# A scaled residual: the first norm's root goes into the merged tiles and x ahead of the output projection

## The chip, the cores and the metric

The kernel runs on one core of a Trainium2 chip. The metric is the device time of one execution in microseconds (us); below 1 us durations are also given in nanoseconds (ns). The kernel before takes 1426.54 us, the median of three runs (1425.07, 1426.54, 1426.93). One execution was recorded by the hardware profiler; it took 1428.4 us, and its span, from the first recorded instruction to the last, is 1426.7 us.

Five engines work side by side, each through its own instructions in order: PE (matrix products), DVE and ACT (element by element), POOL and SP (here they mostly issue DMA transfers: POOL the stores, SP the loads). PEld is PE's loading of the stationary operand.

## The reference, cut to what matters

One decoder layer over x of 1024 tokens by 1024 channels, in float32:

```
u = rms_norm(x, norm1_g)
z_pool, z_lru, z_gelu, z_gate = split(u @ w_in)
y_pool = causal_multiscale_pool(z_pool) @ pool_proj
y_lru  = rglru_branch(z_lru, z_gelu) @ lru_proj
gates  = sigmoid(z_gate + b_gate)                       # two gates per channel
merged = gates[0] * y_pool + gates[1] * y_lru
h = x + merged @ w_out
v = rms_norm(h, norm2_g)
g_ff, u_ff = split(v @ w_ffn_in)
h = h + (silu(g_ff) * u_ff) @ w_ffn_out
h = h + sigmoid(rms_norm(h, ple_norm_g) @ w_ple_gate) * (p @ w_ple_proj)
return rms_norm(h, final_g)

rms_norm(x, g) = x * rsqrt(mean(x * x, over channels) + 1e-6) * g
```

## The kernel before, in words

**Layout.** Activations lie transposed: a tile has 128 channels on the partitions and the 1024 tokens beside one another, in float32; LOW and HIGH are its halves of 512 tokens. A row vector over the tokens, such as a norm's root, is spread to all partitions by PE (`spread`, L367: 16 small matmuls) and copied by ACT (L371) into a tile of the tag `rstd`; `rep1` is that of the first norm, `rep2` that of the second. `norm1.r` and `n2.r` are small columns with the roots themselves.

**Products in two parts.** Every operand of PE is kept as a hi part, which ACT makes by a cast (`hi`, L115), and a lo part, the rest, which DVE makes by a subtraction behind that cast (`lo`, L119). A product takes three matmuls: L219, L220 and L221 (L227 in plain projections). L220 needs the activation's lo part, L221 the weight's. A Strassen scheme with seven products runs over pairs of tiles; a unit is 12 matmuls (k = 0 to 3, three each) over the four operands of one kind: B11, T1, T2, B21, T3, B22, T4 in that order. The operands of T1, T2, T4 and the weight sums come from DVE first (L194 for weights, L400 to L406 for activations). Products that make up one output go to ACT (copies `z`, L497 to L509) and DVE (adds L499 to L507).

**Stages.** Input projection; pooling and LRU branches; the LRU's projection (L227, eight tiles, `done_lru(m)` behind each: two multiplications L933 of the gate with the PE bank, an add L934: merged tile m); the output projection (two groups of two pairs of tiles, 14 units each, 561 to 657 us), the input projection of the channel mixer (`w_fin`), its output projection (`w_fout`, three chunks), and the end with the embedding gate and the last norm.

**The residual.** When an output tile m of the output projection is finished, `residual(m)` adds it to x, loaded by SP into a tile `xr` (L970, DVE), stores the sum, makes `v` from it, the sum times `norm2_g` and `rep1` (L974, DVE), puts the making of `v`'s operands into the background, and adds the square (L327, ACT) to `ss` (L328, DVE; the first tile's square is written to `ss` itself, L324). The second norm's root is taken from `ss` at the sixth product of the next stage; `ratio` (L1001, L1002) divides the first norm's root out again, which is in `v` already.

**What sets the order.** The program is written out when it is built, and each engine keeps that order. `drive` goes through the units: for each it first issues the loads of later weights on SP, then the lo part (`second`) and the hi part (`first`) of weights up to three units ahead, then some steps of the background, then the unit's matmuls, and at the next unit what follows on them (`post`: copies, adds, residuals). The background is a queue of small generators of which the first two are stepped in turn, by a credit of 0.5 us per us of PE work; `some_operands(acts, k, names)` is one, and makes the operands named for one k as soon as its tiles are there. What is not made so early is made by `prepare`, one kind ahead of its use. `force(key)` steps the background until something has been issued.

**The last projection.** In chunk 1 of `w_fout` the class `Residual` loads the stored sums into `hr` and adds them (L1082) when the seventh product of a tile is in. The bank additions are L1079.

Of the kernel before, what the change touches and what calls it, by code (L numbers as in the profile page):

```python
# [64 lines left out]
def hybrid_block(ctx: ExitStack, tc: tile.TileContext, xT, pT, vec, w_in, w_rgig, w_pool,  # L65
# [264 lines left out]
    class Rstd:  # L330
# [8 lines left out]
        def sums(self, last=None):  # L339

            n = self.n
            m = ps()
            for i in range(n):
                t = self.t0 + i * P
                pe.matmul(m[:, i:i + 1], self.ss[:, t:t + P], mean, start=True, stop=last is None)
                if last is not None:
                    pe.matmul(m[:, i:i + 1], last[:, i * P:(i + 1) * P], mean, start=False, stop=True)
            sm = cp.tile([P, 3, 8], F32, name="sm", tag="sm", bufs=3)
            v, r, t = (sm[:, i, :n] for i in range(3))
            dve.tensor_scalar(v, m[:, :n], EPS, None, ALU.add)  # L350
            act.activation(t, v, AF.Sqrt)
            dve.reciprocal(r, t)
            dve.tensor_mul(t, r, r)
            dve.tensor_mul(t, t, v)
            dve.tensor_scalar(t, t, -0.5, 1.5, ALU.mult, ALU.add)
            dve.tensor_mul(r, r, t)
            self.v, self.r = v, r
# [562 lines left out]

    def pre_lru(m, a):
        if m == 0 and a == 0:
            force(*[("y", "op", c) for c in range(4)])
            load_gate(8)
# [5 lines left out]
    def done_lru(m, banks):  # L930
# [3 lines left out]
        dve.tensor_add(g, g, t0.pop(m))  # L934
        if m % 2 == 0:
            ma.a[m // 2] = g
            background.append(some_operands(ma, m // 2, ("B11", "T1")))
        else:
            ma.b[m // 2] = g
            background.append(some_operands(ma, m // 2, ("T2", "B21")))  # L940
# [8 lines left out]
    def load_xr(m):  # L949
        xr[m] = at("xr")  # L950
        nc.sync.dma_start(xr[m], xT[m])
# [3 lines left out]
    def loads_of_group(m0):  # L955
        def pre(q, j, size):
            i = QS.index(q)
            if m0 == 0:
                if i == 0 and j == 0:
                    state["ss2"] = at("ss")  # L960
                    state["rep1"] = norm1.spread()
# [5 lines left out]
    def residual(m):  # L967
        def then(z):
# [3 lines left out]

            v = at("v")
            dve.scalar_tensor_tensor(v, h, col(C_G2, m), state["rep1"], ALU.mult, ALU.mult)  # L974
# [20 lines left out]
    def pre_fin(q, j, size):  # L995
        prepare_v(q, j, size)
        if q == 5 and j == 0:
            state["norm2"].sums()
            n2 = state["norm2"]
            ratio = cp.tile([P, 8], F32, name="ratio")  # L1000
            dve.reciprocal(ratio, norm1.r)  # L1001
            dve.tensor_mul(ratio, ratio, n2.r)  # L1002
            state["ratio"] = ratio
        if q == 7 and j == 0:
            state["rep2"] = state["norm2"].spread(state["ratio"])
# [53 lines left out]
    class Residual:  # L1059
# [12 lines left out]
        def __call__(self, q, bank):  # L1072
            h = hs[2 * self.i], hs[2 * self.i + 1]
            for t, s in {1: ((0, LOW),), 2: ((0, LOW),), 6: ((0, HIGH),), 3: ((0, HIGH),),
# [6 lines left out]
                if not self.left[t] and self.c == 1:  # L1081
                    dve.tensor_add(h[t], h[t], self.h[t])  # L1082
# [39 lines left out]
    for c, (k0, k1) in enumerate(CHUNKS):  # L1122
        def pre_fout(q, j, size, c=c):
            chunks[c].load_some()

# [160 lines left out]
```

## Time and profile before

| | |
|---|---|
| median of three runs | 1426.54 us |
| profiled execution, its span | 1428.4 us, 1426.7 us |
| PE busy | 1363.4 us, 96% |
| DVE busy | 1074.8 us, 75% |
| ACT busy | 697.7 us, 49% |
| output projection, 561 to 700 us | PE 119.14 us busy, mean clock 0.94 |
| DMA moved | 220.56 MB |

How to read it: busy times are sums over instructions, and PE's are modelled at their ends, so a busy PE need not be at its peak. The clock is what was granted of 2.4 GHz, as a share; 0.50 is 1.2 GHz. In a timeline a row has its start, its duration, the engine and line, the operation with out<-in, the shape, a count if several rows are joined, and in brackets how long the engine was idle before it and what ended that. Starts of neighbours on one engine lie closer together than their durations say, since they overlap a little.

### The profile page before, as it was taken

What the parts mean: (1) busy time and instruction counts of PE and PEld (TensorE: products, weight loads), DVE (VectorE), ACT (ScalarE), POOL (GpSimd) and SP (SyncE); (2) the same over time, 40 slices, a digit from 0 to 9 for tenths busy, and PEclk for the clock granted to TensorE, in tenths of its full rate; (3) what the DMA queues carried; (4) which work ended last, traced back from release to release, by engine and by line L of the source; (5) the groups of instructions that cost most, each with busy time, mean ns of one, the idle gap of its engine ahead of it and who ended that gap; (6) DMA issues with size and microseconds to landing.
All of it is one profiled execution on the core that took longest, in us unless ns stands there. A gap on an engine that the chain in (4) does not pass through costs nothing.

```text
span 1426.7 us, 16476 instructions
## 1 busy us (share of the span) xinstructions
PE 1363.4 (96%) x5958; PEld 1117.1 (78%) x5958; DVE 1074.8 (75%) x1583; ACT 697.7 (49%) x1114; POOL 86.5 (6%) x194
## 2 busy tenths in 40 slices
PE   6999999999999999977999999999999999999986
PEld 4787888888788888756788888888888877887865
DVE  5977788888775556778798888888787856768566
ACT  6558665877866122443554444444444521226331
POOL 0003010010000000000001000111110100000000
PEclk7999999999999999989999999999999999999997
DMA  7122143333559221332024444444567798813103
GB/s 311 74 78 97 58 153 110 122 124 109 193 197 364 89 89 38 110 138 98 16 89 148 148 162 148 162 163 163 192 233 268 277 419 303 343 66 126 62 28 118
DMA packets 64738, 220.56 MB, mean 155 GB/s; under 512 B 7312, under 2 KB 9872, under 8 KB 64656
## 3 DMA queue, kind: packets, MB, share of 16 engines
q1 hardware_dynamic: 45936, 151.80, 30.0%
q0 software_dynamic: 18576, 67.64, 11.7%
q8 instruction: 47, 0.77, 0.2%
q14 instruction: 35, 0.29, 0.1%
q10 hardware_dynamic: 144, 0.06, 0.0%
HBM read 147.65 MB, written 71.83 MB: 154 GB/s over the span
## 4 chain that ended last, share of the span: by engine, by line
PE 78%; DVE 11%; ACT 5%; issue 3%; DMA 2%; POOL 1%; DVEq 0%; SPq 0%; ACTq 0%; POOLq 0%
PE ps L221 22%; PE ps L220 22%; PE ps L219 22%; PE ps L227 11%; DVE w L119 2%; DVE ss L328 1%; DVE v L974 1%; DMA wr<-w_fout 1%; DVE xr L970 1%; DMA lT<-fT 1%; DVE wr L194 1%; PE ps L367 1%; DVE xB L119 1%; ACT w L115 1%; DVE xT L119 1%
## 5 line engine op out<-in xcount | busy, mean ns | idle before, releaser
L115 ACT CAST w<-wr 128x512 fp32r<-128x512 f32 (+2 forms) x384 | 227.1, 609 | 362.6 <-DVE wr L194 252.2
L119 DVE TENSOR_TENSOR w<-wr,w 128x512 fp32r<-128x512 f32 (+2 forms) x384 | 256.5, 672 | 52.6 <-ACT w L115 51.9
L221 PE MATMUL ps<-xT,w 128*128 128x512 f32 x704 | 276.3, 392 | 9.9 <-DVE w L119 9.9
L220 PE MATMUL ps<-xT,w 128*128 128x512 f32 x704 | 275.9, 392 | 3.4 <-DVE xT L119 3.4
L219 PE MATMUL ps<-xT,w 128*128 128x512 f32 x704 | 276.0, 392 | 0.1
L220 PE MATMUL ps<-xB,w 128*128 128x512 f32 x528 | 207.6, 393 | 9.3 <-DVE xB L119 9.1
L219 PE MATMUL ps<-xB,w 128*128 128x512 f32 x528 | 206.7, 392 | 2.1 <-ACT xB L115 1.2
L221 PE MATMUL ps<-xB,w 128*128 128x512 f32 x528 | 206.9, 392 | 0.0
L221 PEld LDWEIGHTS ps<-xT,w 128*128 128x128 f32 x704 | 133.1, 189 | 40.3 <-DVE w L119 12.7
L220 PEld LDWEIGHTS ps<-xT,w 128*128 128x128 f32 x704 | 133.1, 189 | 32.5 <-DVE xT L119 5.0
L219 PEld LDWEIGHTS ps<-xT,w 128*128 128x128 f32 x704 | 133.1, 189 | 28.4 <-ACT w L115 0.7
L220 PEld LDWEIGHTS ps<-xB,w 128*128 128x128 f32 x528 | 99.8, 189 | 32.2 <-DVE xB L119 11.8
L219 PEld LDWEIGHTS ps<-xB,w 128*128 128x128 f32 x528 | 99.8, 189 | 23.8 <-ACT xB L115 1.6
L221 PEld LDWEIGHTS ps<-xB,w 128*128 128x128 f32 x528 | 100.0, 189 | 21.1 <-DVE w L119 0.6
L227 PE MATMUL ps<-y,w 128*128 128x512 f32 x384 | 87.2, 389 | 0.0
L227 PEld LDWEIGHTS ps<-y,w 128*128 128x128 f32 x384 | 72.1, 188 | 15.0
L1079 DVE TENSOR_TENSOR h<-h,ps 128x512 f32<-128x512 f32 x68 | 46.5, 684 | 42.6 <-PE ps L221 42.4
L194 DVE TENSOR_TENSOR wr<-wr 128x512 f32<-128x512 f32 (+1 forms) x112 | 76.0, 679 | 3.1 <-DMA wr<-w_fout 1.1
L219 PE MATMUL ps<-lT,w 128*128 128x512 f32 x176 | 68.9, 392 | 3.4 <-DMA lT<-fT 2.6
L221 PE MATMUL ps<-lT,w 128*128 128x512 f32 x176 | 68.7, 390 | 0.0
L220 PE MATMUL ps<-lT,w 128*128 128x512 f32 x176 | 68.5, 389 | 0.0
L115 ACT CAST w<-s 128x512 fp32r<-128x512 f32 (+1 forms) x56 | 34.3, 613 | 57.3 <-DVE s L194 57.3
(218 smaller groups left out, 2145.0 us busy)
## 6 DMA issues: line engine op xcount, KB each, us to landing
wr<-w_fin SPq DMA_DIRECT2D x44, 512.0 KB, 5.7
fT<-xT POOLq DMA_DIRECT2D x44, 512.0 KB, 5.2
lT<-fT SPq DMA_DIRECT2D x44, 512.0 KB, 8.7
wr<-w_in SPq DMA_DIRECT2D x36, 512.0 KB, 4.1
fB<-xB POOLq DMA_DIRECT2D x33, 512.0 KB, 5.7
lB<-fB SPq DMA_DIRECT2D x33, 512.0 KB, 7.7
g<-z POOLq DMA_DIRECT2D x16, 512.0 KB, 2.9
g<-g SPq DMA_DIRECT2D x16, 512.0 KB, 6.4
```

Of the source, the lines that this page charges most:

```text
L115: act.copy(op[:, :x.shape[1]], x)
L119: dve.tensor_tensor(op[:, H:H + n], x, op[:, :n].bitcast(F32), ALU.subtract)
L194: f(self.place(out), self.place(a), self.place(b))
L219: pe.matmul(bank, a, xop[:, :H], start=first, stop=False, skip_group_check=more)
L220: pe.matmul(bank, a, xop[:, H:], start=False, stop=False, skip_group_check=more)
L221: pe.matmul(bank, b, xop[:, :H], start=False, stop=last, skip_group_check=more)
L227: pe.matmul(bank, w, xop[:, s], start=f, stop=e)
L328: dve.tensor_add(ss, ss, sq)
L367: pe.matmul(bank[:, i * P:(i + 1) * P], r[:, b + i:b + i + 1].broadcast_to([P, P]), ident, start=True, stop=True)
L970: dve.tensor_add(h, h, z)
L974: dve.scalar_tensor_tensor(v, h, col(C_G2, m), state["rep1"], ALU.mult, ALU.mult)
L1079: dve.tensor_add(h[t][:, s], h[t][:, s], bank)
```

## The change

The root of the first norm is multiplied into the merged tiles (`done_lru`, new L959) and into x (`scaled_x`, new L932) ahead of the output projection. x is scaled tile by tile in the background, each tile loaded once more, multiplied and stored to DRAM (`xs`), from where the residual loads it. The residual's sum is thus scaled, its square goes into the second norm, with the epsilon scaled by the root's square (`eps1`), `ratio` is not needed any more, and `v` is the sum times `norm2_g` alone, made by ACT (new L1002). In chunk 1 of the last projection the stored sum is multiplied by the inverse root (`inv1`, new L1105) before it is added. The first norm's root is spread at the start of the LRU projection and not at the start of the output projection. Of each odd merged tile the T3 operand is now made in the background too.

```diff
--- before.py
+++ after.py
@@ -336,7 +336,7 @@
         def __init__(self, ss, t0=0, t1=T):
             self.ss, self.t0, self.t1, self.n = ss, t0, t1, (t1 - t0) // P
 
-        def sums(self, last=None):
+        def sums(self, last=None, eps=None):
 
             n = self.n
             m = ps()
@@ -347,7 +347,10 @@
                     pe.matmul(m[:, i:i + 1], last[:, i * P:(i + 1) * P], mean, start=False, stop=True)
             sm = cp.tile([P, 3, 8], F32, name="sm", tag="sm", bufs=3)
             v, r, t = (sm[:, i, :n] for i in range(3))
-            dve.tensor_scalar(v, m[:, :n], EPS, None, ALU.add)
+            if eps is None:
+                dve.tensor_scalar(v, m[:, :n], EPS, None, ALU.add)
+            else:
+                dve.tensor_add(v, eps, m[:, :n])
             act.activation(t, v, AF.Sqrt)
             dve.reciprocal(r, t)
             dve.tensor_mul(t, r, r)
@@ -918,8 +921,29 @@
 
     ma = Acts()
 
+    xs_spill = [spill(f"xs{m}") for m in range(KD)]
+
+    def scaled_x(m):
+
+        x = at("xr")
+        nc.sync.dma_start(x, xT[m])
+        yield None
+        yield None
+        dve.tensor_mul(x, x, state["rep1"])
+        store(xs_spill[m], x)
+        have.add(("xs", m))
+        yield 1.3
+
     def pre_lru(m, a):
         if m == 0 and a == 0:
+
+
+            state["rep1"] = norm1.spread()
+            eps1 = cp.tile([P, 2, 8], F32, name="eps1")
+            state["eps1"], state["rms1"] = eps1[:, 0, :], eps1[:, 1, :]
+            dve.tensor_mul(state["eps1"], norm1.r, norm1.r)
+            dve.tensor_scalar(state["eps1"], state["eps1"], EPS, None, ALU.mult)
+            dve.reciprocal(state["rms1"], norm1.r)
             force(*[("y", "op", c) for c in range(4)])
             load_gate(8)
         if m == 0 and a == 4:
@@ -932,12 +956,15 @@
         for b, s in zip(banks, (LOW, HIGH)):
             dve.tensor_mul(g[:, s], g[:, s], b)
         dve.tensor_add(g, g, t0.pop(m))
+        dve.tensor_mul(g, g, state["rep1"])
+        if m >= 2:
+            background.append(scaled_x(m - 2))
         if m % 2 == 0:
             ma.a[m // 2] = g
             background.append(some_operands(ma, m // 2, ("B11", "T1")))
         else:
             ma.b[m // 2] = g
-            background.append(some_operands(ma, m // 2, ("T2", "B21")))
+            background.append(some_operands(ma, m // 2, ("T2", "B21", "T3")))
 
     plain([w_lru[m] for m in range(KD)], KD, lambda: ys, done_lru, pre_lru, 2)
 
@@ -948,7 +975,8 @@
 
     def load_xr(m):
         xr[m] = at("xr")
-        nc.sync.dma_start(xr[m], xT[m])
+        force(("xs", m))
+        nc.sync.dma_start(xr[m], xs_spill[m])
 
     prepare_m = prepare(ma)
 
@@ -958,7 +986,8 @@
             if m0 == 0:
                 if i == 0 and j == 0:
                     state["ss2"] = at("ss")
-                    state["rep1"] = norm1.spread()
+                    background.append(scaled_x(KD - 2))
+                    background.append(scaled_x(KD - 1))
                 prepare_m(q, j, size)
             if j == 0 and i in (2, 3, 4, 5):
                 load_xr(m0 + {2: 0, 3: 2, 4: 1, 5: 3}[i])
@@ -969,9 +998,8 @@
             h = xr.pop(m)
             dve.tensor_add(h, h, z)
             store(h_spill[m], h)
-
             v = at("v")
-            dve.scalar_tensor_tensor(v, h, col(C_G2, m), state["rep1"], ALU.mult, ALU.mult)
+            act.activation(v, h, AF.Copy, scale=col(C_G2, m))
             if m % 2 == 0:
                 va.a[m // 2] = v
                 background.append(some_operands(va, m // 2, ("B11", "T1")))
@@ -995,14 +1023,9 @@
     def pre_fin(q, j, size):
         prepare_v(q, j, size)
         if q == 5 and j == 0:
-            state["norm2"].sums()
-            n2 = state["norm2"]
-            ratio = cp.tile([P, 8], F32, name="ratio")
-            dve.reciprocal(ratio, norm1.r)
-            dve.tensor_mul(ratio, ratio, n2.r)
-            state["ratio"] = ratio
+            state["norm2"].sums(eps=state["eps1"])
         if q == 7 and j == 0:
-            state["rep2"] = state["norm2"].spread(state["ratio"])
+            state["rep2"] = state["norm2"].spread()
         if q == 4:
             have.add("va")
 
@@ -1079,6 +1102,7 @@
                     dve.tensor_add(h[t][:, s], h[t][:, s], bank)
                 self.left[t] -= 1
                 if not self.left[t] and self.c == 1:
+                    dve.tensor_mul(self.h[t], self.h[t], state["inv1"])
                     dve.tensor_add(h[t], h[t], self.h[t])
                 if not self.left[t] and self.c == len(CHUNKS) - 1:
                     complete.append(2 * self.i + t)
@@ -1122,6 +1146,8 @@
     for c, (k0, k1) in enumerate(CHUNKS):
         def pre_fout(q, j, size, c=c):
             chunks[c].load_some()
+            if c == 1 and q == QS[0] and j == 0:
+                state["inv1"] = norm1.spread(state["rms1"])
 
         strassen(chunks[c], [(w_fout[2 * i, :, k0 * 2 * P:k1 * 2 * P],
                               w_fout[2 * i + 1, :, k0 * 2 * P:k1 * 2 * P]) for i in range(KD // 2)],
```

Where it moves instructions: first DVE, at the second residual of the output projection's first group (`xr`, `v` and `ss` are the tiles named above; `w` and `wr` are a weight's operand and its tile). Before:

```order
L503 TENSOR_TENSOR z<-z,ps 128x512
L970 TENSOR_TENSOR xr<-xr,z 128x1024
L974 SCALAR_TENSOR_TENSOR v<-xr,cv,rstd 128x1024
L328 TENSOR_TENSOR ss<-ss,sq 128x1024
L119 TENSOR_TENSOR w<-wr,w 128x512
L194 TENSOR_TENSOR wr<-wr 128x512 x2
```

And DVE at the same residual now:

```order
L506 TENSOR_TENSOR z<-z,ps 128x512
L999 TENSOR_TENSOR xr<-xr,z 128x1024
L328 TENSOR_TENSOR ss<-ss,sq 128x1024
L119 TENSOR_TENSOR w<-wr,w 128x512
L194 TENSOR_TENSOR wr<-wr 128x512 x2
L119 TENSOR_TENSOR xB_4819<-v,xB_4819 128x512
```

The row of `v` is gone from DVE, and `ss` stands right behind `xr`, in all seven residuals that have one.

Next ACT, at the same residual (`cv` is the column of `norm2_g`, `xB` and `xT` are operands of the next stage). Before:

```order
L115 CAST xB_4767<-v 128x512
L327 ACTIVATE sq<-xr 128x1024
L115 CAST w<-wr 128x512
L115 CAST xB_4795<-v 128x512
L115 CAST xT_4798<-v 128x512
L509 COPY z<-ps 128x512
```

And ACT there now:

```order
L115 CAST xB_4819<-v 128x512
L1002 ACTIVATE v<-xr,cv 128x1024
L327 ACTIVATE sq<-xr 128x1024
L115 CAST w<-wr 128x512
L115 CAST xB_4847<-v 128x512
L115 CAST xT_4850<-v 128x512
L512 COPY z<-ps 128x512
```

The Copy that makes `v` stands between `xr` and the square.

Last ACT at the head of the output projection, from the casts made during the last LRU units to the first copy of a finished product (`z`). Before, `xB_4425` is the B11 operand of k=3, made from merged tile 6, `s_4490` a weight sum:

```order
L115 CAST xB_4425<-g 128x512
L115 CAST w<-wr 128x512
L115 CAST xT_4460<-g 128x512
L115 CAST w<-s_4490 128x512
L371 COPY rstd<-ps 128x512 x2
L115 CAST xT_4511<-g 128x512
L497 COPY z<-ps 128x512
```

And ACT there now, where `xB_4542` is that operand of k=3 and `s_4537` the weight sum:

```order
L115 CAST xT_4433<-g 128x512
L115 CAST w<-wr 128x512
L115 CAST xT_4473<-g 128x512
L115 CAST w<-wr 128x512
L115 CAST w<-s_4537 128x512
L115 CAST xB_4542<-g 128x512
L115 CAST xB_4546<-g 128x512
L500 COPY z<-ps 128x512
```

The operand of k=3 has moved behind the cast of the weight sum, and that sum stands on DVE behind the whole of `done_lru(7)` and one lo half.

## Rows read from the trace of the kernel before

**Rows 1.** Page, part 1: busy us of each engine (share of span), instructions.

```profile
PE 1363.4 (96%) x5958; PEld 1117.1 (78%) x5958; DVE 1074.8 (75%) x1583; ACT 697.7 (49%) x1114; POOL 86.5 (6%) x194
```

**Rows 2.** Stretches: length, busy us of each engine (instructions), PE clock, DMA share, GB/s.

```profile
540.00:560.00 20.00, 20.00 (x90) 16.56 (x89) 13.65 (x20) 4.05 (x7) 0.00 (x0) 1.00 0.03 7
561.00:700.00 139.00, 119.14 (x508) 95.83 (x507) 110.24 (x160) 64.10 (x110) 4.25 (x8) 0.94 0.27 95
700.00:1040.00 340.00, 339.68 (x1507) 281.40 (x1506) 285.53 (x426) 151.48 (x257) 29.76 (x56) 1.00 0.41 146
615.20:618.50 3.30, 3.30 (x10) 2.53 (x8) 3.30 (x6) 1.59 (x3) 0.00 (x0) 0.51 0.00 0
623.60:628.50 4.90, 4.88 (x12) 3.82 (x13) 4.12 (x7) 2.84 (x6) 0.00 (x0) 0.50 0.30 107
666.50:669.60 3.10, 3.10 (x7) 2.47 (x8) 2.53 (x5) 1.73 (x4) 0.00 (x0) 0.50 0.00 0
```

**Rows 3.** PE's timeline: start, duration, instruction, [idle before <-what ended it].

```profile
614.35 0.50 PE L221 MATMUL ps<-xT,w 128*128 128x512 f32 x1 [3.79 <-DVE w L119]
623.62 0.80 PE L221 MATMUL ps<-xT,w 128*128 128x512 f32 x1 [4.64 <-DVE w L119]
666.49 0.80 PE L220 MATMUL ps<-xB,w 128*128 128x512 f32 x1 [7.19 <-DVE xB L119]
```

**Rows 4.** DVE's timeline, the second residual of the first group and a weight.

```profile
601.78 1.23 DVE L970 TENSOR_TENSOR xr<-xr,z 128x1024 f32<-128x1024 f32 x1
603.04 1.28 DVE L974 SCALAR_TENSOR_TENSOR v<-xr,cv,rstd 128x1024 f32<-128x1024 f32 x1
604.24 1.22 DVE L328 TENSOR_TENSOR ss<-ss,sq 128x1024 f32<-128x1024 f32 x1
613.61 0.68 DVE L119 TENSOR_TENSOR w<-wr,w 128x512 fp32r<-128x512 f32 x1
```

**Rows 5.** ACT's timeline, squares beside `v`, and what follows one.

```profile
603.10 1.06 ACT L327 ACTIVATE sq<-xr 128x1024 f32<-128x1024 f32 x1 [2.15 <-DVE xr L970]
649.79 1.06 ACT L327 ACTIVATE sq<-xr 128x1024 f32<-128x1024 f32 x1 [8.81 <-DVE xr L970]
650.75 0.61 ACT L115 CAST w<-wr 128x512 fp32r<-128x512 f32 x1
```

**Rows 6.** ACT's groups by form: count, busy us, mean ns, idle before.

```profile
L133 ACT ACTIVATE v<-h,cv 128x512 fp32r<-128x512 f32 x16 | 10.9, 717 | 9.2 <-DVE h L1079 9.2
L115 ACT CAST w<-wr 128x512 fp32r<-128x512 f32 x352 | 212.3, 620 | 342.1 <-DVE wr L194 238.2 <-issue 33.7 <-PE ps L221 28.5
L327 ACT ACTIVATE sq<-xr 128x1024 f32<-128x1024 f32 x7 | 7.4, 1060 | 19.0 <-DVE xr L970 19.0
L658 ACT ACTIVATE xc<-z,cv 128x1024 f32<-128x1024 f32 x8 | 10.0, 1250 | 0.0
```

**Rows 7.** DVE's and PE's timelines at the head of the output projection.

```profile
560.91 1.28 DVE L933 TENSOR_TENSOR g<-g,ps 128x512 f32<-128x512 f32 x2 [2.32 <-PE ps L227]
562.23 1.23 DVE L934 TENSOR_TENSOR g<-g 128x1024 f32<-128x1024 f32 x1
562.64 0.48 PE L219 MATMUL ps<-xB,w 128*128 128x512 f32 x1
572.25 0.69 DVE L119 TENSOR_TENSOR w<-wr,w 128x512 fp32r<-128x512 f32 x1 [1.55 <-ACT w L115]
583.80 1.98 DVE L119 TENSOR_TENSOR xT<-g,xT 128x512 fp32r<-128x512 f32 x3
```

**Rows 8.** PE's spread; PE's waits (us, times, longest); a DMA group of the page.

```profile
560.93 1.95 PE L367 MATMUL ps<-ident,sm 128*128 128x128 f32 x16
PE ps L219 <- DMA lT<-fT: 2.6, 2, 1.5
fT<-xT POOLq DMA_DIRECT2D x44, 512.0 KB, 5.2
```

**Rows 9.** DVE's groups by form.

```profile
L713 DVE TENSOR_SCALAR th<-th 128x1024 f32<-128x1024 f32 x8 | 5.5, 694 | 0.3
```

## The prediction

> **What bounds the kernel now.** I began with the page's busy shares: PE is busy 96% of the span [rows 1], so a change of DVE, ACT and DMA work can only move the time through what PE loses. Next came the table of stretches, to find where it loses. In the output projection, 561 to 700 us, PE is busy 119.14 of 139 us at a mean clock of 0.94; in the input projection of the channel mixer behind it, 339.68 of 340 at 1.00 [rows 2]. The first is the stage that the change rewrites, and it holds the loss: 19.9 us idle, and beside it three pieces of 3.3, 4.9 and 3.1 us at a granted clock of 0.51 or 0.50 [rows 2], the lower level (1.2 GHz), which cost half their length, 5.7 us. About 25 us is thus the most that any gain there can be.
>
> Third, PE's own timeline says who ends these gaps [rows 3]: DVE each time, by the lo half of a weight (`w` L119) or of an activation operand (`xT`, `xB` L119). Each piece at the low clock lies right behind a gap of 3.79, 4.64 or 7.19 us. Fourth, DVE's timeline shows why its lo halves are late [rows 4]. A finished tile of the projection sets off a residual: `xr` L970 (1.23 us), `v` L974 (1.28), `ss` L328 (1.22), and only then the weight's `w` L119; the one that starts at 613.61 is the one that PE gets at 614.35. DVE does not pause inside: starts at 601.78, 603.04, 604.24. The square that `ss` adds is made by ACT beside `v`, from 603.10 to 604.16 [rows 5], just in time for `ss` at 604.24.
>
> **The change part by part.**
>
> *The scaling of `v` goes to ACT.* DVE loses 8 rows of 1.28 us; by their starts each took 1.20 (603.04 to 604.24). ACT gains 8 Copies with a per-partition scale, and ACT's order puts each ahead of the residual's Square. The trace has no such Copy of 128x1024. Nearest rows [rows 6]: the same form at 128x512 takes 717 ns against 620 for a cast without the scale, so the scale costs some 0.10; a Square of 128x1024 takes 1060; together 1.16. Identity with scale and bias takes 1250. I take 1.16, within 1.06 and 1.25. What matters is the wait. `ss` stands right behind `xr` on DVE now, and needs the Square, which stands behind `v`. From the start of `xr`: ACT starts at +1.32 (601.78 to 603.10), the Square +1.06 later (1.16, less the 0.10 by which ACT's instructions overlap: 649.79 to 650.75 is 0.96 for 1.06 [rows 5]), it lasts 1.06, and `ss` starts 0.05 behind, at +3.49. Before it was +2.46. So each of the 7 residuals that have an `ss` puts DVE 1.03 later (0.93 to 1.12 over the price of the Copy), idle where it worked. Were the Copy free, `ss` would start at +2.43: nothing would be gained even then. Queued behind `ss` are `w` L119 and the operands for which PE waits. In the first group three residuals follow one another up to the gaps at 614.35 and 623.62, in the second four, up to 666.49 and the stage's end. Sum: 7 x 1.03 = **+7.2**. The first residual has no `ss` and lets its `w` go 1.20 earlier.
>
> *Merged tiles multiplied, operands in a new order.* Eight `g` multiplications (L959), each at the price of the add before it [rows 7], 1.23, by starts 1.14. Seven lie in the LRU projection, where DVE is busy 13.65 of 20 us and PE waits for none of it [rows 2]. The eighth stands at the head of the output projection. Before, the operand of merged tile 6 (k=3 of the first two units) was cast before DVE came to the last tile (`g` L933 at 560.91), and PE ran unit 0 from 562.64 without a gap. Now ACT's order has it behind a cast of `s_4537`, and that sum DVE makes only after the last tile's two multiplications, its add and the new multiplication. With the old durations: PE still ends the LRU units at 562.6 (the 16 spread matmuls, 1.71 us [rows 8], are now ahead of them); DVE then takes 1.32 for two multiplications, 1.26 for the add, 1.14 for the new multiplication, 0.60 for a lo half and 0.69 for the sum, to 567.7; ACT two casts (0.53 + 0.62) to 568.9; and PE gets k=3 there instead of 2.1 behind its start, at 564.7. For the lo half it waits 0.7 more. Unit 0 ends at 570.1 instead of 565.4: **+4.7**. The gap is of the size that brought the low clock at 614.35, so half of 3.3 us: **+1.7**. If ACT's queue ran ahead the term is 0; with a full piece such as the 4.9 it is 8.
>
> *x scaled early.* Eight loads on SP, eight DVE multiplications (L932, 1.14 by starts), eight stores on POOL, and the residual's load now takes the stored tile: 16 more transfers of 512 KB. They run where the DMA share is 0.03 and 0.27 [rows 2], so I cost them at nothing; SP is in order, so if one waited for a store, the weights behind it would be late by about one transfer, 5.2 us for a store on POOL [rows 8]. Four multiplications fall into the LRU stage, four into the first group, 4 x 1.14 = +4.6 on DVE. The early T3 operands take three lo halves out of the first group (the row of 583.80 shows three in 1.98 us [rows 7]): -1.9. With the first residual's -1.2 this leaves +1.5, of which DVE's idle stretches behind the first units (1.55 at 572.25 [rows 7], shortened by what unit 0 is late) take about one multiplication. Taken: **+0.5**, bounds -3.1 (all four hidden) and +2.7 (none hidden, the first `v` not counted).
>
> *Norms and the last projection.* `ratio` goes, two DVE rows of 0.19 and 0.17: -0.3. In chunk 1 of the output of the channel mixer 16 spread matmuls are new, 1.71 us on PE [rows 8]; chunk 1 has 2.6 us of waits for `lT` from DMA [rows 8], which can take it up: +0.5, between 0 and 1.7. Eight multiplications `hr` (L1105, 1.14 each) come in two clusters of four; I take 0, since PE waits there for DMA and not for DVE [rows 8], and +4.6 as the bound, if one cluster holds up PE's banks.
>
> **The sum.** 7.2 + 4.7 + 1.7 + 0.5 - 0.3 + 0.5 = +14.3. Against the profiled execution (span 1426.7, 1428.4 us in all) this is 1442.7; that execution lies 1.9 above the median of the three runs, 1426.54, so by the median **about 1441 us**. With the prices of the Copy alone the term of 7.2 runs from 6.5 to 7.8; the likeliest case by itself spans 1436 to 1446.
>
> One rule speaks against the change. The row of L713 has an operation of one tensor and a scalar (a maximum) on DVE, 128x1024, at 694 ns [rows 9], a little over half of `v`'s 1.28 with two tensor inputs. The Trainium skill, VectorE: DVE Perf Modes, section Rules for kernel authors, says to do multiplications on VectorE and not on ScalarE, and its tier table lets a one-source float32 op run at twice the rate of a two-source one; the trace agrees. Once the root is out of `v`, by this rule `v` would stay on DVE at 0.69, `ss` would start no later than before, and the sum would lose its 7.2 and come to about 1434. The diff sends it to ACT, so the sum stands.
>
> **Rivals.**
>
> *A, not slower: DVE was the bound, and it has less to do.* PE's gaps in this stage end on DVE [rows 3]; 8 x 1.20 of `v` and 1.9 of T3 leave it, two multiplications of 1.14 come where it is full: -9.2, so 1417.3, or some 1420 if unit 0 waits a little. It decides if the Square is done within 1.2 us of the end of `xr`; the price of the Copy and ACT's order speak against it, since `ss` then starts at +3.49. Chance 0.11.
>
> *B, one of the two mechanisms is hidden.* Either unit 0 doesn't wait (ACT gets the sum's cast off in time), or PE's new lateness runs beside the residuals' waits, so that DVE finds its tiles later anyway and the two do not add. Then +14.3 loses about 7: 1434. For it: DVE is idle for 1.55 us at a time behind the first units [rows 7]. Against it: from the first residual on DVE does not pause [rows 4], so that what comes late stays late. Chance 0.22.
>
> *C, more waits.* The clusters of chunk 1 hold PE (+4.6), or an SP load waits for a store of `xs` (+5.2): about 1446, or 1450 with both. For it: SP has the weights behind those loads. Against it: no wait for these additions is among PE's, and the DMA share ahead of the residuals is low [rows 2]. Chance 0.11.
>
> *D, nothing.* The added waits fall into gaps that PE had anyway: within 0.2% (2.9 us, about what a measurement of this kernel can tell from no change), 1426 to 1429. The gaps are ended by the very rows that come later, which leaves this 0.08.
>
> **How the numbers follow.** The forecast has 0.48, B 0.22, C 0.11, A 0.11, D 0.08. Slower by over 0.2% is forecast, B and C: 0.81. The range goes from 1428, where D ends, up to 1450, C; it leaves out A and part of D.
>
> **What would show it.** In the new profile: on DVE an idle of about 2.3 us ahead of each of seven `ss` rows, ended by ACT `sq`; on PE a wait of about 4 us in unit 0 of the output projection, ended by ACT `xB` L115, and a piece at the lower clock behind it; the gaps of 3.79 and 7.19 about 1 to 2.5 us longer; no new wait for DMA; the rest of the program shifted as a block from 700 us on. The forecast is wrong if `ss` starts less than 3 us behind `xr`, if unit 0 runs through, or if the stage from its first unit to its last lasts less than 145 us (before 561 to 700).

## The result and the profile after

The changed kernel takes 1447.78 us (median of four runs, 1446.76 to 1449.54), the kernel before, on the same chip, 1426.74: a ratio of 1.0149 [1.0136, 1.0161] (in brackets, here and below, the 95% interval), some 21 us more. The forecast was 1441 within 1428 to 1450. Direction and range held; the likeliest time is 6.8 us short, and the measured one lies just outside the 1436 to 1446 that the prediction gave its likeliest case.

Where the 21 us lie is read from the same five rows in both traces: PE's first unit of the output projection, ACT's first and last activation on the channel mixer's gate (`fg<-fg`, called `fg` below), the first square that ACT writes to `sq` for the last norms, and the end. The second stretch holds, besides the output projection, the first units of the mixer's input projection; it is called the output projection in what follows.

| stretch | before | after | more |
|---|---|---|---|
| up to unit 0 of the output projection | 562.6 | 563.0 | 0.4 |
| unit 0 to the first `fg` (output projection) | 165.0 | 179.1 | 14.1 |
| first to last `fg` (input projection of the mixer) | 368.8 | 368.8 | 0.0 |
| last `fg` to the first square (last projection) | 195.8 | 200.9 | 5.1 |
| from there to the end | 134.5 | 135.6 | 1.2 |

The page's first part, as in [rows 1]. DVE, from which `v` was taken, has more to do, not less:

```profile
PE 1374.5 (95%) x5974; PEld 1124.6 (78%) x5974; DVE 1092.2 (75%) x1600; ACT 707.4 (49%) x1124; POOL 90.7 (6%) x202
```

The stretches that answer to those of [rows 2], moved by 14 to 15 us and with the stage's new length; behind them three stretches at the lower clock (columns as there: length, busy us of PE, PEld, DVE, ACT, POOL, clock, DMA share, GB/s):

```profile
561.00:715.00 154.00, 125.37 (x503) 99.22 (x502) 109.44 (x161) 73.16 (x118) 6.38 (x12) 0.89 0.32 115
715.00:1055.00 340.00, 339.69 (x1507) 281.42 (x1506) 285.42 (x426) 151.96 (x258) 29.76 (x56) 1.00 0.40 146
569.20:573.80 4.60, 4.58 (x10) 3.37 (x11) 3.91 (x7) 2.76 (x5) 0.00 (x0) 0.50 0.01 4
624.70:629.30 4.60, 4.56 (x11) 3.59 (x12) 4.29 (x7) 2.01 (x4) 0.00 (x0) 0.50 0.00 0
680.40:683.50 3.10, 3.09 (x7) 2.48 (x8) 2.53 (x5) 1.71 (x4) 0.00 (x0) 0.50 0.00 0
```

The channel mixer's input projection runs as before, without a gap. The output projection is longer, and its clock is lower.

PE's longest gaps there; the third, fourth and last answer to [rows 3]:

```profile
569.23 0.80 PE L219 MATMUL ps<-xB,w 128*128 128x512 f32 x1 [4.00 <-ACT xB L115]
607.13 0.51 PE L220 MATMUL ps<-xT,w 128*128 128x512 f32 x1 [2.70 <-DVE xT L119]
624.74 0.80 PE L221 MATMUL ps<-xT,w 128*128 128x512 f32 x1 [4.39 <-DVE w L119]
634.91 0.80 PE L221 MATMUL ps<-xT,w 128*128 128x512 f32 x1 [4.99 <-DVE w L119]
671.32 0.50 PE L220 MATMUL ps<-xB,w 128*128 128x512 f32 x1 [2.86 <-DVE xB L119]
680.41 0.80 PE L220 MATMUL ps<-xB,w 128*128 128x512 f32 x1 [8.11 <-DVE xB L119]
```

The wait of 4.00 is new; 3.79, 4.64 and 7.19 have become 4.39, 4.99 and 8.11, and the 2.86 was 0.87 before (at 658.33). PE's waits over the whole program (sum in us, times, longest), after:

```profile
PE ps L221 <- DVE w L119: 15.7, 9, 5.0
PE ps L220 <- DVE xB L119: 12.2, 5, 8.1
PE ps L219 <- ACT xB L115: 5.2, 2, 4.0
PE ps L220 <- DVE xT L119: 4.2, 4, 2.7
PE ps L219 <- DMA lT<-fT: 3.5, 4, 1.6
```

and the same lines before:

```profile
PE ps L221 <- DVE w L119: 13.9, 7, 4.6
PE ps L220 <- DVE xB L119: 9.1, 4, 7.2
PE ps L219 <- ACT xB L115: 1.2, 1, 1.2
PE ps L220 <- DVE xT L119: 3.4, 4, 2.4
```

The first four lines are 37.3 against 27.6 over the whole program. In the stretch of the output projection alone PE is idle 28.9 us against 20.2: +8.8. The pieces at 0.50 in which PE works are five now, 22.0 us together by its rows (569.2 to 574.8, 609.1 to 612.4, 624.7 to 629.4, 634.9 to 639.7, 680.4 to 684.0); before there were three, which by the same reading last 12.1 (615.2 to 618.7, 623.6 to 628.9, 666.5 to 669.9), a little more than the stretches of [rows 2]. Half the difference is +4.9. Idle and clock together make 13.7 of the 14.1.

DVE's residual, to lay beside [rows 4]:

```profile
610.44 1.22 DVE L999 TENSOR_TENSOR xr<-xr,z 128x1024 f32<-128x1024 f32 x1
613.83 1.23 DVE L328 TENSOR_TENSOR ss<-ss,sq 128x1024 f32<-128x1024 f32 x1 [2.17 <-ACT sq L327]
614.97 0.69 DVE L119 TENSOR_TENSOR w<-wr,w 128x512 fp32r<-128x512 f32 x1
```

and ACT beside it, as in [rows 5]:

```profile
611.70 1.15 ACT L1002 ACTIVATE v<-xr,cv 128x1024 f32<-128x1024 f32 x1 [2.09 <-DVE xr L999]
612.75 1.04 ACT L327 ACTIVATE sq<-xr 128x1024 f32<-128x1024 f32 x1
```

The square starts only at 612.75, when the Copy is all but done (611.70 and 1.15), and DVE stands still for 2.17 us with the weight's `w` queued behind `ss`. There are seven such waits, 2.16 to 2.23 us each.

The head of the output projection, DVE and then ACT (before: [rows 7]):

```profile
565.57 1.23 DVE L959 TENSOR_TENSOR g<-g,rstd 128x1024 f32<-128x1024 f32 x1
566.72 0.68 DVE L119 TENSOR_TENSOR w<-wr,w 128x512 fp32r<-128x512 f32 x1
567.32 0.68 DVE L194 TENSOR_TENSOR s<-wr 128x512 f32<-128x512 f32 x1
```

```profile
568.04 0.62 ACT L115 CAST w<-s 128x512 fp32r<-128x512 f32 x1 [4.48 <-DVE s L194]
568.56 1.13 ACT L115 CAST xB<-g 128x512 fp32r<-128x512 f32 x2
```

ACT idles 4.48 us for a weight sum of a later unit, and the cast for which PE waits stands behind it.

### The profile page after: what moved, and what is told of

Read it like the earlier page. It is cut to its first block, busy times and chain, and to the rows that moved or that the text cites. A ratio compares the mean times of both kernels' runs of the same rounds, so it can differ in the third digit from the quotient of the medians.

```text
span 1447.5 us, 16572 instructions
## 1 busy us (share of the span) xinstructions
PE 1374.5 (95%) x5974; PEld 1124.6 (78%) x5974; DVE 1092.2 (75%) x1600; ACT 707.4 (49%) x1124; POOL 90.7 (6%) x202
## 4 chain that ended last, share of the span: by engine, by line
PE 72%; DVE 12%; ACT 6%; DMA 4%; issue 4%; POOL 1%; DVEq 0%; ACTq 0%; SPq 0%; POOLq 0%
PE ps L221 20%; PE ps L220 20%; PE ps L219 20%; PE ps L227 10%; DMA lT<-fT 2%; DVE w L119 2%; DVE ss L328 1%; DVE wr L194 1%; DMA hr<-h 1%; ACT sq L327 1%; DMA wr<-w_fout 1%; DVE xr L999 1%; ACT w L115 1%; PE ps L370 1%; DVE xB L119 1%
## 5 line engine op out<-in xcount | busy, mean ns | idle before, releaser
L219 PEld LDWEIGHTS ps<-xT,w 128*128 128x128 f32 x704 | 133.7, 190 | 28.9 <-ACT xT L115 0.8
L219 PE MATMUL ps<-lT,w 128*128 128x512 f32 x176 | 70.3, 399 | 3.5 <-DMA lT<-fT 3.5
L221 PE MATMUL ps<-lT,w 128*128 128x512 f32 x176 | 69.7, 396 | 0.4 <-DVE w L119 0.4
L220 PE MATMUL ps<-lT,w 128*128 128x512 f32 x176 | 69.6, 396 | 0.0
```

Source lines behind the costliest of these rows:

```text
L219: pe.matmul(bank, a, xop[:, :H], start=first, stop=False, skip_group_check=more)
L220: pe.matmul(bank, a, xop[:, H:], start=False, stop=False, skip_group_check=more)
L221: pe.matmul(bank, b, xop[:, :H], start=False, stop=last, skip_group_check=more)
```

## The experiments

Each ratio below is to the kernel before, run in turn on the same chip. The stages are those of the table above, from each kernel's profile, which is one execution. Three dots in a cut of code stand for lines left out.

**The square ahead of `v` on ACT.** Nothing but the order of two instructions, eight times.

```diff
             v = at("v")
+            add_square(h, state["ss2"], m == 0)
             act.activation(v, h, AF.Copy, scale=col(C_G2, m))
...
-            add_square(h, state["ss2"], m == 0)
```

> The changed kernel (1447.8 us) with the residual's Square ahead of the Copy that makes v on ACT; everything else, DVE's order too, is as it was. Theory W (the order on ACT makes ss wait): ss starts 1.05 us earlier behind xr in each of seven residuals (3.39 to about 2.35), v is ready 1 us later but still before DVE comes to its operands; 7 x 1.05 = 7.4, so about 1440.5. Rival L (DVE's and the DMA queues' added load, 24 multiplications and 16 transfers, makes the loss, whatever the order): the load is the same, so 1446 to 1448.

Measured: 1438.19 us, 1.0073 [1.0061, 1.0086]. The output projection takes 171.6 us, 7.5 less than in the changed kernel.

```profile
609.43 1.23 DVE L999 TENSOR_TENSOR xr<-xr,z 128x1024 f32<-128x1024 f32 x1
611.78 1.22 DVE L328 TENSOR_TENSOR ss<-ss,sq 128x1024 f32<-128x1024 f32 x1 [1.12 <-ACT sq L327]
```

`ss` starts 2.35 us behind `xr` and no longer 3.39. DVE is idle there still, 1.12 us in this row, for it has no `v` to fill the time.

**`v` on DVE, as an operation of one tensor and a column.**

```diff
-            act.activation(v, h, AF.Copy, scale=col(C_G2, m))
+            dve.tensor_scalar(v, h, col(C_G2, m), None, ALU.mult)
```

> The changed kernel with v made on DVE by one tensor and a scalar (0.69 us by the row of L713 of before) in place of ACT's Copy. Theory W: ss starts 2.4 us behind xr as it did before the change, the idle time ahead of it falls from 2.2 to 0.5 us; 7 x 1.0 = 7, less 0.6 for the first residual's w: about 1441. Rival L: eight more rows of 0.60 on a DVE that is the bound: 1448 to 1452.

Measured: 1438.25 us, 1.0073 [1.006, 1.0086], the output projection 172.1.

```profile
608.55 1.23 DVE L999 TENSOR_TENSOR xr<-xr,z 128x1024 f32<-128x1024 f32 x1
609.81 0.75 DVE L1002 TENSOR_SCALAR v<-xr,cv 128x1024 f32<-128x1024 f32 x1
610.96 1.23 DVE L328 TENSOR_TENSOR ss<-ss,sq 128x1024 f32<-128x1024 f32 x1 [0.40 <-ACT sq L327]
```

`ss` starts at +2.41. Two different edits bring `ss` forward by the same 1.0 us and give the same time, though the second one adds work to DVE: the wait for the square is 7 to 7.5 us of the stage.

**The operand of k=3 made inside `done_lru(7)`, ahead of its work.**

```diff
     def done_lru(m, banks):
+        if m == KD - 1:
+            ma.run("B11", 3, 0)
+            ma.run("B11", 3, 1)
```

> The changed kernel with the B11 operand of k=3 issued ahead of the last merged tile's DVE work, as it came before the change. Theory W: the wait of 4.0 us in unit 0 of the output projection, the 0.4 behind it and the piece at the lower clock after it go; 4.7 + 1.7 = 6.4, of which the next units give a part back in waits for weight sums: 1441 to 1443. Rival L, or that what PE gains there is lost again at the residuals, since DVE is as full as it was: 1446 to 1448.

Measured: 1443.67 us, 1.0109 [1.0095, 1.0124], the output projection 176.1, so 3.0 less. Unit 0 runs through; in the third unit PE waits instead for the operand of the other kind:

```profile
571.31 0.50 PE L219 MATMUL ps<-xT,w 128*128 128x512 f32 x1 [2.40 <-ACT xT L115]
```

The wait is where the prediction has it, but a good half of the 6.4 us that it was to cost comes back: this wait, 3.4 us at the lower clock behind it (572.4 to 575.8), and longer gaps at the first residuals (5.23 and 5.85 for 4.39 and 4.99). The time is a little above the 1441 to 1443 expected.

**Without the inverse root in chunk 1:** neither the 16 spread matmuls nor the eight multiplications `hr`; the stored sum is added unscaled.

```diff
-                    dve.tensor_mul(self.h[t], self.h[t], state["inv1"])
...
-            if c == 1 and q == QS[0] and j == 0:
-                state["inv1"] = norm1.spread(state["rms1"])
```

> The changed kernel without the inverse root: neither its spread on PE nor the eight multiplications of hr in chunk 1 of the last projection (the stored sum is added unscaled). In the profile the last projection grew by 5.1 us: spread 1.7, waits for lT and lB 4.2 instead of 3.3, and a piece of 5.7 us at the lower clock. Theory W (the spread and what follows on it): all of it goes, -5, so about 1442.7. Rival S (only the spread's own 1.7 belongs to it, the rest is the DMA queue, which the moved stages have shifted): about 1446.

Measured: 1446.06 us, 1.013 [1.0116, 1.0144], the rival's time and not the 1442.7 of the theory: 1.7 us come back by the medians (the intervals overlap), 1.0 in the last projection of the profile (200.0 us); the spread takes 1.7 [rows 8]. What it keeps:

```profile
1199.83 0.50 PE L219 MATMUL ps<-lT,w 128*128 128x512 f32 x1 [1.34 <-DMA lT<-fT]
1202.36 0.80 PE L219 MATMUL ps<-lT,w 128*128 128x512 f32 x1 [1.57 <-DMA lT<-fT]
```

The DMA waits are there without the inverse root, and so is the lower clock behind them (the matmul of 0.80).

**The scaled x stored in the places of the sums,** so that no place in DRAM is added ahead of the spilled tiles `f`.

```diff
-    xs_spill = [spill(f"xs{m}") for m in range(KD)]
+    h_spill = [spill(f"h{m}") for m in range(KD)]
+    xs_spill = h_spill
...
-    h_spill = [spill(f"h{m}") for m in range(KD)]
```

> The changed kernel with the scaled x stored in the places that the residual's sums take later, so that no place in DRAM is added and every tile that the last projection loads lies at the address it had before the change. In the traces the loads of the last projection, while they alone keep the DMA engines full, move some 410 GB/s after the change and 418 before it, with or without the inverse root, and PE waits 4.2 us for them and not 3.3, with a piece of 5.7 us at the lower clock behind the two last waits. Theory P (the 4 MB more of places, which shift all later tiles, cost that rate): waits back to 3.3, no low clock, about -3.7, so 1444. Rival Q (places are nothing; the load and store order around the stage makes it): 1447 to 1448, 410 GB/s again.

Measured: 1446.28 us, 1.0139 [1.0123, 1.0156]. The loads of the last projection, a stretch of 10 us of the kernel before, of the changed one and of this one (the last column is GB/s):

```profile
1174.00:1184.00 10.00, 9.39 (x41) 7.15 (x39) 5.96 (x9) 1.24 (x2) 0.00 (x0) 1.00 1.02 419
```

```profile
1174.00:1184.00 10.00, 10.00 (x46) 8.28 (x45) 8.50 (x15) 3.45 (x7) 0.00 (x0) 1.00 1.02 407
```

```profile
1174.00:1184.00 10.00, 10.00 (x45) 8.28 (x45) 8.37 (x14) 3.14 (x6) 0.00 (x0) 1.00 1.02 407
```

The engines of the DMA are full in all three; in the changed kernel and in this one they move 3% less. The added places in DRAM are not the reason. The last projection takes 199.0 us in this profile, 1.9 less than in the changed kernel: the waits are still there (1.30 and 1.56 at the end), but the piece at 0.50 behind them lasts 2.9 us in place of 5.9.

**x not scaled:** the residual adds x as it is, so that the root is missing from x; the eight loads, multiplications and stores of `scaled_x` are gone.

```diff
-        if m >= 2:
-            background.append(scaled_x(m - 2))
...
-        force(("xs", m))
-        nc.sync.dma_start(xr[m], xs_spill[m])
+        nc.sync.dma_start(xr[m], xT[m])
...
-                    background.append(scaled_x(KD - 2))
-                    background.append(scaled_x(KD - 1))
```

> The changed kernel without the scaling of x: the residual adds x as it is, loaded as before the change (this leaves the root out of x); the eight multiplications, eight loads and eight stores are gone, and the B11 operand of k=3 comes ahead of the weight sum again. Theory W: unit 0 waits less (4.0 us of ACT wait gone, some of the lo half's kept), -4 to -6; the multiplications in the first group -1; the places in DRAM as before, -3.7 if theory P of the run beside it holds. The seven waits of ss stay. About 1438, without P 1442. Rival L (the added load and transfers make most of the loss): 1428 to 1432.

Measured: 1437.63 us, 1.0077 [1.0063, 1.009]. The output projection takes 169.3 us, 9.8 less: 4.0 less idle time of PE, and 10.4 us at the lower clock in place of 22.0, half of which is 5.8. The last projection, at 200.5, keeps its excess, and its loads run at 407 to 409 GB/s. In the stage the wait in unit 0 is gone although the eighth `g` multiplication is still made at 565.80. ACT shows why:

```profile
558.68 0.61 ACT L115 CAST xB<-g 128x512 fp32r<-128x512 f32 x1
568.32 0.62 ACT L115 CAST w<-s 128x512 fp32r<-128x512 f32 x1 [5.03 <-DVE s L194]
```

The operand of k=3 is cast ahead of the weight sum again, with the multiplication of the merged tiles still in place. What had pushed it behind were the steps of `scaled_x` in the background queue: only two generators are stepped in turn, by a credit, and the operand waited for its place.

**The addition `ss` issued later:** kept back and issued ahead of the next residual's `xr`, the last one ahead of the second norm's sums. With the early operand of k=3.

```diff
             h = xr.pop(m)
+            while late_ss:
+                late_ss.popleft()()
             dve.tensor_add(h, h, z)
...
-            add_square(h, state["ss2"], m == 0)
...
+                sq = at("sq")
+                act.activation(sq, h, AF.Square)
+                late_ss.append(lambda: dve.tensor_add(state["ss2"], state["ss2"], sq))
...
+            while late_ss:
+                late_ss.popleft()()
             state["norm2"].sums(eps=state["eps1"])
```

> The changed kernel with two edits: the B11 operand of k=3 early (1443.7 by itself), and the addition to ss issued ahead of the next residual's xr and not behind its own, so that DVE goes on to the weight at once and finds the Square done. Theory W (what DVE waits for and does ahead of the weight sets PE's gaps): the weight's lo half starts 3.4 us earlier behind xr, the addition of 1.14 comes back ahead of the next xr, where DVE has 0.6 to 1.2 us idle; seven times 2.3 is 16, less where another operand then decides: 1428 to 1433, on DVE no idle ended by ACT sq. Rival V (PE's gaps are set by v, which comes from ACT 1.15 us behind xr, and its operands): 1438 to 1442.

Measured: 1439.12 us, 1.0079 [1.0061, 1.0097], where 1428 to 1433 was expected; the time is that of the rival, the wait is not. I had not thought of the last `ss`: nothing hurries it, and the second norm's sums on PE wait for it.

```profile
679.32 3.58 PE L345 MATMUL ps<-mean,ss 128*128 128x1 f32 x16 [7.73 <-DVE ss L1021]
```

**The same with the scaled x in the places of the sums.** Edit: this and that of the fifth experiment.

> All three edits together: the B11 operand early, the addition to ss deferred, the scaled x in the places of the residual's sums. It computes the whole layer. If W and P both hold: what defer_ss takes, less 3.7: 1425 to 1429, at or a little below the kernel before. If P fails it equals defer_ss; if W's second half fails, 1436 to 1440.

Measured: 1437.11 us, 1.0074 [1.0059, 1.0089], with a wait of 7.82 us for the last `ss`. The places in DRAM make no difference here either that stands clear of the intervals.

**The kernel before once more,** only to see whether the load rate and the last projection of one profile are an accident.

```diff
+# again
```

> The kernel before, unchanged, with a second profile. In the first one the loads of the last projection moved 420 GB/s to their end at 1184 us, and no low clock followed on the two last waits for lT; in all eight profiles of changed kernels they fall to about 410 GB/s after 20 us, the waits grow by 0.3 to 1 us, and a piece at the lower clock follows. Theory E (that is a matter of the change: something in its order or timing): again 420 GB/s, 195.8 us from the last Silu to the first Square of the third norm. Rival F (it differs from execution to execution, whatever the kernel): 410 GB/s and 198 to 200 us in this profile, and no more than 2 us between its runs and the first ones'.

Measured: 1428.53 us, 1.0001 [0.9993, 1.001]; the last projection 195.7 us (195.8 in the first profile), loads again at 418 to 420 GB/s. The stage takes 195.5 to 195.8 us in the three profiles of the kernel before and its variant, and 198.2 to 201.0 in the eleven of the changed kernel and its variants: the excess belongs to the change.

**The kernel before with `ss` issued later,** all but the last, which stays where it was. It keeps `v` on DVE and the norm as it was.

```diff
+            while late_ss:
+                late_ss.popleft()()
             dve.tensor_add(h, h, z)
...
+                if m == KD - 1:
+                    dve.tensor_add(state["ss2"], state["ss2"], sq)
+                else:
+                    late_ss.append(lambda: dve.tensor_add(state["ss2"], state["ss2"], sq))
```

> The kernel before with one edit: the addition to ss is issued ahead of the next residual's xr and not behind its own v (the last one stays where it was). Nothing is taken from DVE's work. Theory W (what stands between xr and the weight's lo half on DVE sets PE's gaps): the weight and the operands behind it come 1.14 us earlier in six residuals, the addition falls where DVE is idle 0.6 to 1.2 us ahead of xr: -3 to -6 with the shorter gaps' clock, 1420 to 1424. Rival L (DVE's sum of work counts): 1426.

Measured: 1423.04 us, 0.9963 [0.995, 0.9975]: faster than both kernels. The output projection takes 160.9 us against 165.0.

```profile
600.68 1.23 DVE L974 TENSOR_TENSOR xr<-xr,z 128x1024 f32<-128x1024 f32 x1
601.94 1.29 DVE L978 SCALAR_TENSOR_TENSOR v<-xr,cv,rstd 128x1024 f32<-128x1024 f32 x1
603.14 0.68 DVE L119 TENSOR_TENSOR w<-wr,w 128x512 fp32r<-128x512 f32 x1
```

The weight's lo half follows `v`, 2.46 us behind `xr`; in [rows 4] `ss` stood there.

**The changed kernel with both lessons:** `ss` later except the last, B11 and T1 of k=3 made ahead of the last merged tile.

```diff
     def done_lru(m, banks):
+        if m == KD - 1:
+            ma.run("B11", 3, 0)
+            ma.run("B11", 3, 1)
+            ma.run("T1", 3, 0)
+            ma.run("T1", 3, 1)
...
+                if m == KD - 1:
+                    dve.tensor_add(state["ss2"], state["ss2"], sq)
+                else:
+                    late_ss.append(lambda: dve.tensor_add(state["ss2"], state["ss2"], sq))
```

> The changed kernel with B11 and T1 of k=3 early and the additions to ss deferred, but for the last one. defer_ss (1439.1) had a new wait of 7.7 us of the second norm's sums for the last ss, and one of 2.4 for xT in the third unit. Theory W: both go, a wait of about 2.2 us for the last Square comes: 1430 to 1433. Rival V (v from ACT sets the gaps): the sums' wait turns into one for operands, 1437 to 1440.

Measured: 1425.16 us, 0.998 [0.9965, 0.9994], better than the 1430 to 1433 expected. The output projection takes 159.6 us, 19.5 less than in the changed kernel and 5.4 less than before. The wait for the second norm's sums is 0.51 us. T1 made early does not take the wait for `xT` away: in place of the 2.40 in the third unit stands one of 2.60 at 577.32, which no lower clock follows. How much the last `ss` gives and how much T1 no run separates. The last projection, at 199.7, keeps its excess.

**That kernel with `v` on DVE.**

```diff
-            act.activation(v, h, AF.Copy, scale=col(C_G2, m))
+            dve.tensor_scalar(v, h, col(C_G2, m), None, ALU.mult)
```

> As the run beside it, with v on DVE by one tensor and a scalar (0.69 us). Theory W: DVE has 0.60 more ahead of each weight, but v is there 0.5 us earlier and the last ss waits less: within 2 us of the run beside it. Under rival V it is 2 to 4 us faster than that.

Measured: 1432.18 us, 1.0026 [1.0015, 1.0038], 7 us slower than with `v` on ACT, where both theories had it within 2 us or faster. Of the 5.3 us by which the two profiled executions differ, the output projection has 2.4 (162.0 against 159.6: 3.9 more idle time of PE, 2.0 less at the lower clock); 1.2 lie ahead of it, where the two kernels are the same, and 1.8 behind it. PE waits longer for a weight's lo half behind the first residuals; first the row of this kernel, then that of the one with `v` on ACT:

```profile
623.81 0.80 PE L221 MATMUL ps<-xT,w 128*128 128x512 f32 x1 [4.30 <-DVE w L119]
```

```profile
620.17 0.50 PE L221 MATMUL ps<-xT,w 128*128 128x512 f32 x1 [2.10 <-DVE w L119]
```

Both gaps are followed by the lower clock: the longer one at once, until 629.0, the shorter one 0.8 us later, from 621.0 to 624.4. Why the rest of the 7 us is lost stays open.

## Why the prediction was right, and where its size was off

*The scaling of `v` on ACT* (+7.2): right, by its own steps. The Copy takes 1.15 where 1.16 was worked out, `ss` starts 3.39 behind `xr` where 3.49 was, and seven waits of 2.2 us stand ended by the square. Taking the wait away, with `v` on ACT or on DVE, shortens the stage by 7.5 or 7.0. Not all of it is lateness of DVE handed on to PE, as the term has it: of the 7.5, PE's idle time is some 6.2; the rest is half of the 2.9 us less at the lower clock. The sign that the gaps of 3.79 and 7.19 grow by 1 to 2.5 failed: they grew by 0.60 and 0.92, and the one of 0.87 by 1.99.

*The wait in unit 0* (+4.7, and +1.7 for the clock): right in place and releaser, and nearly in size. It lasts 4.00, and 5.6 us at 0.50 follow, so 2.8 for the clock. (The bound of 8 with a full piece such as the 4.9 does not come out of its parts: 4.7 and half of 4.9 are 7.2.) Its cause was booked on the wrong line: the prediction told it under the merged tiles, and costed the scaling of x at +0.5. Without the scaling the wait is gone and the stage is 9.8 shorter. The bounds of that term (-3.1 to +2.7) were thus too narrow, since they counted DVE's busy time and not the background's places that the new generators take.

*The terms do not add.* The edits for the square, for x and for the early operand give back 7.5, 9.8 and 3.0 of 14.1, more than there is. The last two take away the same wait, and their worth differs by what follows: 24.9 us idle and 10.4 at the lower clock in the one, 27.9 and 18.6 in the other. That the forecast's stage sum (7.2 + 4.7 + 1.7 + 0.5 - 0.3 = 13.8) lies so near the 14.1 is in good part luck. Without the clock's 1.7 it counted 12.1 us of idle time, where PE has 8.8 more; for the clock it counted 1.7, behind unit 0 alone, where it cost 4.9 in the whole stage. The two errors cancel.

*The last projection* (+0.5): this is the term that was mis-sized; it measured +5.1, and two of its signs, no new wait for DMA and the rest shifted as a block, failed. Two parts of the step fell. First, that the waits for DMA would take up the spread: its matmuls run at

```profile
1161.63 1.95 PE L370 MATMUL ps<-ident,eps 128*128 128x128 f32 x16
```

while the waits come 25 to 42 us later, and they are no shorter:

```profile
1187.18 0.50 PE L219 MATMUL ps<-lT,w 128*128 128x512 f32 x1 [0.30 <-DMA lT<-fT]
1201.26 0.50 PE L219 MATMUL ps<-lT,w 128*128 128x512 f32 x1 [1.33 <-DMA lT<-fT]
1203.78 0.80 PE L219 MATMUL ps<-lT,w 128*128 128x512 f32 x1 [1.56 <-DMA lT<-fT]
```

The spread is therefore on the path; leaving it out gave back 1.0 to 1.7. Second, that the DMA part would stay as it was. The waits for `lT` and `lB` sum to 4.18 (five waits) against 3.25 (three), and behind the last two lies a piece at the lower clock that the kernel before does not have:

```profile
1203.80:1209.50 5.70, 5.70 (x14) 4.45 (x14) 4.68 (x6) 0.62 (x1) 0.00 (x0) 0.50 0.28 92
```

Half of 5.7 is 2.8; 1.7 + 0.9 + 2.8 = 5.4, less 0.7 for a wait for ACT that is gone: 4.7 of the 5.1. The size of the last part is not fixed: in five of the ten variants PE works only 2.8 to 3.4 us at 0.50 there, behind last waits of nearly the same length (1.30 to 1.35 and 1.54 to 1.56), and the stage takes 198.2 to 199.2 us, an excess of 2.3 to 3.4. The multiplications `hr`, taken at 0, show no wait of PE. The 1.2 us from the last projection to the end, which the prediction has at nothing, are not traced further.

Why the loads fall behind is not settled. In the changed kernel and its ten variants they start at 417 to 420 GB/s and go on at 407 to 414, read in stretches of 10 us with a share of 1.02 or more; in the kernel before, its second profile and its variant they stay at 418 to 421. It is not the inverse root (the waits stay without it), not the added places in DRAM, and not the 16 transfers of x (407 to 409 without them). Nor is it the order of the transfers: from 24 to 83 us behind the last `fg` the same 40 loads and 9 stores are issued in the same order in all fourteen profiles. Where their tiles lie in SBUF can differ, since all tiles take turns in one pool; no run here isolates that, and the cause stays open.

*Rivals.* A lost on the point that it named: the square was not done within 1.2 us of the end of `xr`, but 2.1 us behind it. Its premise, that DVE's work sets the gaps, shows once `ss` is out of the way: there 0.75 us more per residual come with a stage 2.4 us longer. B would have needed one of the two mechanisms hidden; neither is. C has the nearest time (1446), but neither of its waits: PE waits for no bank behind the `hr` clusters, and though SP's loads do wait for stores (30.8 us in one case, for the store of a sum, 4.8 in another, for one of `xs`), PE waits for no DMA in the output projection. D is ruled out by the interval.

*The rule that spoke against the change.* On DVE `v` takes 0.75 us, against 1.28 with two tensor inputs, and the changed kernel with that one line altered stands at 1.0073 [1.006, 1.0086] of the kernel before, not at 1.0149 [1.0136, 1.0161]. The Trainium skill, ScalarE: Activation LUTs, section Rules for kernel authors, sends a multiplication to VectorE, with a figure that it gives for bf16 (the prediction names the page on VectorE, which has the tier table and not this rule); here the runs agree as long as `ss` waits for a square queued behind `v`, and disagree once it does not, where the kernel with ACT's Copy is the faster one by 1432.18 against 1425.16.

## What to carry to other kernels

Moving an instruction off a busy engine gains nothing if the next one on that engine waits for the engine to which it was moved: look at what stands right behind it, not at busy sums. On an engine that keeps its order, a sum that nobody needs soon belongs behind the work that others wait for, except its last part: here that alone took the kernel before from 1427.94 to 1423.04 us. A new generator in a shared queue costs the places of those behind it, also where its own instructions fall into idle time.

## What the runs showed of the hardware that was not expected

- The same saturated loads, in the same order (DMA share 1.02 to 1.03), run at 418 to 420 GB/s in the kernel before, in both its profiles, and fall to 407 to 411 midway in the changed one.
- In the changed kernel two waits of 1.33 and 1.56 us, 2.5 us apart from start to start of the matmuls behind them, are followed by 5.7 us at a granted clock of 0.50; two of 1.35 and 1.54 at the same distance, in the kernel with the early operand, by 2.8; two of 1.12 and 1.52 (1185.18 and 1187.67 before) by none.
- A Copy with a per-partition scale of 128x1024 float32 on ACT takes 1.13 to 1.15 us, a multiplication by such a column on DVE 0.75.
